# Output projection of the first 1024 tokens beside the recurrence, streamed first down product, heads in turn: a hybrid layer on one Trainium2 core

## Chip, cores and metric

The kernel runs on one core of one Trainium2 chip. The metric is the device time of one execution in microseconds (us). PE is the TensorE (matmul) engine, PEld its weight loads, DVE is VectorE, ACT is ScalarE, POOL is GpSimd, SP is SyncE, which issues most DMAs here.

## What is computed

One layer over 2048 tokens of width 1024, all in float32 at the interface. An input projection feeds three groups side by side (a diagonal state-space layer with 256 outputs, differential attention with 384, a gated linear recurrence with 384). Their 1024 outputs pass one output projection, are added to the residual, and a gated MLP (2816 wide, with a causal convolution over 3 tokens) follows.

```python
h = rmsnorm(x, norm_mix_g[l])
proj = h @ w_in[l]
u, dq, dk, dv, cq, cf, ci, cg = split_projection(proj)
y_a = s5_mixer(u, ...)                  # state space, 256 columns
y_b = diff_attention(dq, dk, dv, ...)   # 6 heads, 384 columns
y_c = hgrn2_mixer(cq, cf, ci, cg, ...)  # 6 heads, 384 columns, chunks of 64
mix = jnp.concatenate([y_a, y_b, y_c], axis=-1)
x = x + mix @ w_out[l]
h = rmsnorm(x, norm_ffn_g[l])
up, gate = h @ w_up, h @ w_gate         # up: then conv over 3 tokens + bias
x = x + (gelu(up) * gate) @ w_down
return rmsnorm(x, final_norm_g)
```

## The kernel before

**Precision.** Large products run in float16 with every operand split into a high and a low half (`Ctx.split`: one ScalarE and one VectorE or GpSimd instruction), and three of the four half products are summed. Matmuls inside the recurrence are float32.

**Two streams of work.** At the end of the kernel, `left()` yields the input projection, then attention in two halves (query tiles 0 to 7 and 8 to 15 of 128 tokens, all six heads each), and `right()` yields the state-space layer, the recurrence (`phase_hgrn`), and the rest (`phase_tail`). `weave` takes the next step from the stream whose summed price is lower. The prices are the six numbers `LW`; those of attention are also multiplied by `K.pace`, which `phase_tail` sets anew by stage. The order in which steps are drawn gives every instruction its priority. The tile framework then fixes each engine's program order when the kernel is built, from these priorities and a plan of when operands and buffers are there. An instruction further back can go first when an earlier one is not ready. `until(n)` draws attention until n head pairs are done.

**Attention.** For a head h and query tile i, `scores` issues one matmul (tile `t_ps`) and one VectorE instruction for each 512 keys and each of two maps: a score chunk. Softmax on ScalarE, a combination on VectorE, a split on ScalarE and GpSimd, transposing DMAs (`t_wt`) on SP's queue, and value matmuls (`t_po`) follow. The second half keeps fewer tiles in flight (`s_bufs` 4).

**Recurrence.** `phase_hgrn` has 12 units: three pairs of heads, four chunks of 512 tokens each. A unit is `proj` (input products, tiles `g_pq`, `g_pv`), `pre` and `fin` (which writes 128 features of 512 tokens to `Yd`). In `pre`, `meet` multiplies 64 rows of partitions (one head of the pair) for 4 blocks of 128 tokens at three levels; L1239 is its matmul. Units overlap, and the last two (10 and 11, tokens 1024 to 2047) are woven with `early_mix` under the name `spare`.

**Output projection.** `Yd` holds eight blocks of 128 features, q numbers pairs of them. `early_mix` takes q = 0, 1, 3 for tokens 0 to 511: it loads and splits six blocks of `w_out` one after another through one staging buffer (`o_wst`), then makes eight output tiles of 128 tokens by 512 columns, 18 matmuls each, in one PSUM bank (`pj`), adds x and stores the result in `Xd`. The tail's `first` adds q = 2 to those tokens (`project(0, ...)`, 48 matmuls) and does tokens 512 to 1023 whole (`project(1, ...)`, 192 matmuls). In the second half of the latter stand the transposes of the first 512 tokens (`turned(xs, left)`). The normed, transposed tokens of `first` fill seven operand tiles `f_q`.

**MLP.** `activations` makes, for half 0 (tokens 0 to 1023) and later half 1, the 22 blocks of the hidden layer. A Strassen-like scheme needs seven products instead of eight in the up projections (`f_pm`, L97), and again in the down product (class `Down`, tile `f_pd`, L1769): step i multiplies a sum of activation blocks (`f_da`, from DRAM) with a sum of blocks of `w_down` (`f_dw`), 132 matmuls a step. For half 0, steps 0 to 3 get their weights by `stage`, which loads pieces of `w_down` through three buffers (`f_dst`) and splits them. For steps 4 to 6, `hold` reserves four whole blocks of `w_down` (`f_db`), `load` fetches them, `sum` combines them on GpSimd in place, and `right` splits. `hold` uses memory of attention, so `before()` draws all attention that is left, at i = 2. `second` projects tokens 1024 to 2047; step 6 of half 0 runs inside it. The up products and the down product of half 1 follow.

In `Down.run`, with `staged` = 4 for half 0, step i prepares step i + 1:

```python
if i == staged - 1 - (staged > 1):
    before()
    self.hold(pooler(e2)("f_db", 1, side))
for b in self.LOADS[self.half].get(i, ()):
    self.load(b)
```

Of the kernel before, what the change touches and what calls it, by code (L numbers as in the profile page):

```python
# [9 lines left out]
F32 = mybir.dt.float32  # L10
# [8 lines left out]
S = 2048  # L19
# [14 lines left out]
EARLY = [0, 1, 3]  # L34
DOWN_PARTS = [3, 3, 3, 2]
MADE = range(0, MF, 2)
LW = [6.0, 0.44, 5.0, 2.5, 0.62, 1.0]
# [974 lines left out]
def phase_hgrn(K, Hd, w_in, lb_logits, norm_g, Yd, spare):  # L1012
# [9 lines left out]
    with ExitStack() as es:  # L1022
# [146 lines left out]
        def pre(u):  # L1169
# [65 lines left out]
            def meet(hl, dd, ps, e, c0):  # L1235
                hh = slice(64 * e, 64 * e + 64)
                for bk in range(NB):
                    tk = dd[hh, 128 * bk:128 * bk + 128]
                    nc.tensor.matmul(  # L1239
                        out=ps[:, c0 + 64 * bk:c0 + 64 * bk + 64].rearrange("p (n y) -> p n y", y=hl),  # L1240
                        lhsT=tk, rhs=tk.rearrange("p (n x y) -> p n x y", x=2, y=hl)[:, :, 1],
                        start=True, stop=True,
                    )
# [9 lines left out]
            for group in ((32, 16), (8,)):  # L1253
# [3 lines left out]
                for i, hl in enumerate(group):  # L1257
                    for e in range(2):
                        meet(hl, ds[i], ps[e], e, 256 * i)
# [112 lines left out]
        yield from weave(rest(), 18, spare(pj, st, wp, hp, w3, w2), 6)  # L1372


def early_mix(K, x, w_out, Yd, Xd, pj, st, wp, hp, w3, w2):

    nc = K.nc
    y = []
    for a in range(2):
        t = hp.tile([128, 2, KD, 256], F16, tag="h", name="o_ye")  # L1380
        for k in [k for q in EARLY for k in (2 * q, 2 * q + 1)]:
            nc.sync.dma_start(out=t[:, :, k], in_=Yd[k, :, :, 256 * a:256 * a + 256])
        y.append(t)
    w4 = wp.tile([128, 4, 2, 2, 512], F16, tag="w", name="o_we")
    ws = [w4[:, i] for i in range(4)]
    ws += [w2.tile([128, 2, 2, 512], F16, tag="x", name="o_wx") for _ in range(2 * len(EARLY) - 4)]
# [9 lines left out]
    for n in range(2):  # L1396
        cc = slice(512 * n, 512 * n + 512)
        for t in range(4):
            rows = slice(128 * t, 128 * t + 128)
            tk = slice(128 * (t % 2), 128 * (t % 2) + 128)  # L1400
            r = w3.tile([128, 512], F32, tag="vn", name="o_re")
            nc.sync.dma_start(out=r, in_=x[0, rows, cc])
            ps = pj.tile([128, 512], F32, tag="j", name="o_pe")
            i = 0
            for q, w in zip(EARLY, ws[len(EARLY) * n:]):
                for k in range(2):
                    for a, b in ((0, 0), (0, 1), (1, 0)):
                        nc.tensor.matmul(
                            out=ps, lhsT=y[t // 2][:, a, 2 * q + k, tk], rhs=w[:, b, k, :],
                            start=(i == 0), stop=(i == 6 * len(EARLY) - 1),  # L1410
                        )
                        i += 1
            nc.vector.scalar_tensor_tensor(
                out=r, in0=ps, scalar=IWS / YS, in1=r, op0=ALU.mult, op1=ALU.add
            )
            nc.sync.dma_start(out=Xd[S + 128 * t:S + 128 * t + 128, cc], in_=r)
            yield 1


def phase_tail(K, x, Xd, Yd, Ad, w_out, norm_g, W, conv_w, conv_b, w_down, final_g, out, es,  # L1420
# [226 lines left out]
    class Down:  # L1647
# [19 lines left out]
        LOADS = ({2: (B12, B11), 3: (B22,), 4: (B21,)}, {0: (B21,), 1: (B22, B11), 2: (B12,)})  # L1667
# [22 lines left out]
        def stage(self, i, st, cs=(0, 1, 2, 3)):  # L1690

            for c in cs:
                q0, n = self.cuts[c]
                w = self.room(i, c)
                for q in range(0, n, 2):
                    k = min(2, n - q)
                    b, pair, _ = self.STEPS[i]
                    fs = []
                    for b in pair or (b,):
# [99 lines left out]
        def run(self, rs, tp, pms, side, staged, before):  # L1799
# [3 lines left out]
            with ExitStack() as e1:  # L1803
                pool = pooler(e1)
                st = pool("f_dst", 3) if staged > 1 else None
                self.more(pool)
                if not self.w:
                    self.ahead(st)
                with ExitStack() as e2:
                    for i in range(6):  # L1810
# [3 lines left out]
                        if i == staged - 1 - (staged > 1):  # L1814
                            before()
                            self.hold(pooler(e2)("f_db", 1, side))
                        for b in self.LOADS[self.half].get(i, ()):
                            self.load(b)
                        if i + 1 < staged:
                            self.stage(i + 1, st)  # L1820
                        else:
                            for c in range(len(self.cuts)):
                                if i + 1 == staged == 4:
                                    self.sum(3, c)
                                self.right(i + 1, c)
# [3 lines left out]
                if self.half == 1:  # L1829
                    yield from self.product(6, pms[6 % len(pms)], True)  # L1830
# [284 lines left out]
```

## Time and profile before

| | us |
|---|---|
| median of three runs | 2770.08 |
| their range | 2767.73 to 2774.96 |
| the profiled execution | 2772.72 |
| its span in the profile | 2771.0 |

A row of the windows view gives, for a stretch of the span, how long each engine was busy, the clock that TensorE was granted (1.00 is full), the busy share of the DMA engines and the GB/s they moved. With a tile's name it counts only instructions that touch that tile, in the same columns for the engines that do. A row of groups gives a source line, engine, operation, names as out<-in, and count, then busy us, mean ns, and idle time before. A row of the timeline or of the chain that ended last begins with the start and the duration in us. Matmul durations overlap: 264 of some 380 ns each may pass in 60 us.

### The profile page before, as it was taken

How to read it: one execution, taken by the hardware profiler on the slowest of the kernel's cores; microseconds unless marked ns; L12 is line 12 of the kernel's file. 1: busy time of each engine (PE TensorE's matmuls, PEld its weight loads, DVE VectorE, ACT ScalarE, POOL GpSimd, SP SyncE). 2: the span in 40 equal slices, each digit the busy share in tenths (PEclk: the TensorE clock that was granted, in tenths of full speed). 3: DMA queues.
4: the chain of work that ended last, by engine and by line, in shares of the span. 5: the costliest groups of instructions: out<-in, count | busy, mean ns of one | idle time of the engine just before them, and what ended most of it. 6: DMA issues, size and time to landing. Idle time of an engine off the chain costs nothing.

```text
span 2771.0 us, 42468 instructions
## 1 busy us (share of the span) xinstructions
PE 2437.1 (88%) x15438; PEld 1374.1 (50%) x15438; DVE 1941.6 (70%) x3497; ACT 1269.5 (46%) x2273; POOL 1362.6 (49%) x1144
## 2 busy tenths in 40 slices
PE   5998889988988888868987988769999999999998
PEld 4655547766766764334443433334344444444444
DVE  7567746888878987688778998963654755555475
ACT  6333344666645654654455665541234433333221
POOL 5787602544444543456667566622902444444280
PEclk8999999988998888879999989979999999999999
DMA  7676554555464656954456555687675655554733
GB/s 245 228 224 194 179 155 112 125 125 123 86 153 97 129 131 142 296 143 129 171 158 177 159 161 146 211 238 239 229 266 178 227 156 150 167 156 135 282 101 122
DMA packets 554531, 474.11 MB, mean 171 GB/s; under 512 B 276880, under 2 KB 432848, under 8 KB 553296
## 3 DMA queue, kind: packets, MB, share of 16 engines
q1 hardware_dynamic: 532144, 431.02, 55.1%
q10 hardware_dynamic: 22176, 40.38, 4.0%
q8 instruction: 121, 1.98, 0.3%
q14 instruction: 90, 0.74, 0.1%
HBM read 289.30 MB, written 127.93 MB: 151 GB/s over the span
## 4 chain that ended last, share of the span: by engine, by line
PE 36%; DVE 15%; DMA 9%; issue 8%; ACT 6%; POOL 5%; SPq 1%; ACTq 0%; DVEq 0%; POOLq 0%
PE f_pm L97 15%; PE f_pd L1769 10%; PE o_pm L1486 3%; DVE t_sc L837 3%; DMA t_wt<-t_sc 2%; DVE t_sc L868 2%; ACT t_sc L849 2%; DMA f_dst<-in_w_down_dram 2%; PE g_pq L97 2%; DMA o_y<-Yd 1%; PE g_pv L97 1%; POOL t_sc L892 1%; DVE f_w L64 1%; DVE f_t L1610 1%; DVE f_a L62 1%
## 5 line engine op out<-in xcount | busy, mean ns | idle before, releaser
L97 PE MATMUL f_pm<-f_q,f_w 128*128 128x512 f16 x3696 | 844.3, 388 | 43.3 <-DVE f_u L1834 24.9
L97 PEld LDWEIGHTS <-f_w 128*128 128x128 f16 x3696 | 364.3, 100 | 501.1 <-issue 80.5
L1769 PE MATMUL f_pd<-f_dw,f_da 128*128 128x512 f16 x1848 | 408.7, 384 | 15.1 <-DVE f_r L1747 10.2
L892 POOL TENSOR_TENSOR t_sc<-t_sc 128x1024 f16<-128x1024 f32 (+7 forms) x144 | 253.6, 1774 | 278.8 <-ACT t_sc L891 220.9
L1769 PEld LDWEIGHTS <-f_da 128*128 128x128 f16 x1848 | 182.4, 99 | 238.0 <-issue 23.0
L849 ACT ACTIVATE t_sc<-t_sc,t_nm 128x128 f32<-128x128 f32 (+7 forms) x192 | 229.0, 1194 | 77.7 <-DVE t_nm L844 69.8
L833 PE MATMUL t_ps<-t_k,t_q 96*128 96x512 f16 (+2 forms) x480 | 167.3, 374 | 93.0 <-DVE t_mx L837 84.1
L837 DVE CUSTOM_DVE_ANT_0 t_sc<-t_ps,t_base,t_mx 128x512 f32<-128x512 f32 (+3 forms) x288 | 185.2, 645 | 26.9 <-PE t_ps L833 17.1
L62 DVE TENSOR_TENSOR f_a<-f_t,f_a 128x512 f16<-128x512 f32 x132 | 158.3, 1219 | 50.1 <-ACT f_a L56 49.6
L914 PEld LDWEIGHTS <-t_wt 128*128 128x128 f16 x2448 | 107.9, 103 | 117.7 <-DMA t_wt<-t_sc 50.1
L868 DVE SCALAR_TENSOR_TENSOR t_sc<-t_sc,t_a 128x1024 f32<-128x1024 f32 (+7 forms) x144 | 164.9, 1170 | 1.1
L97 PE MATMUL g_pv<-g_w,g_h 128*128 128x256 f16 x1152 | 157.1, 294 | 9.1 <-ACT g_w L56 8.1
L1834 POOL TENSOR_TENSOR f_t<-f_t,f_t 128x512 f32<-128x512 f32 x66 | 101.9, 1557 | 126.9 <-ACT f_a L56 91.6
L1486 PE MATMUL o_pm<-o_w,o_y 128*128 128x512 f16 x624 | 144.1, 389 | 20.8 <-DMA o_y<-Yd 10.4
L97 PE MATMUL g_pq<-g_h,g_w 128*128 128x256 f16 x1152 | 156.7, 292 | 6.0 <-DVE g_sg L1161 3.9
L914 PE MATMUL t_po<-t_v,t_wt 128*128 128x64 f16 x2448 | 122.6, 200 | 40.7 <-DMA t_wt<-t_sc 35.4
L1834 POOL TENSOR_TENSOR f_db<-f_db 128x1536 f32<-128x1536 f32 (+1 forms) x32 | 128.1, 4041 | 56.0 <-DMA f_db<-in_w_down_dram 56.0
L64 DVE SCALAR_TENSOR_TENSOR f_dw<-f_db,f_dw 128x1536 f16<-128x1536 f32 (+1 forms) x36 | 103.3, 2898 | 71.7 <-ACT f_dw L56 71.7
L891 ACT CAST t_sc<-t_sc 128x1024 f16<-128x1024 f32 (+7 forms) x144 | 111.2, 793 | 86.6 <-DVE t_sc L868 82.9
L1834 POOL TENSOR_TENSOR f_k<-f_k,f_k 128x512 f32<-128x512 f32 x88 | 124.6, 1416 | 51.0 <-ACT f_halo L1878 25.2
L1610 DVE SCALAR_TENSOR_TENSOR f_t<-f_u,f_cw,f_t 128x1024 f32<-128x1024 f32 x88 | 125.8, 1429 | 32.6 <-ACT f_t L1608 32.3
L837 DVE CUSTOM_DVE_ANT_0 t_sc<-t_ps,t_base 128x512 f32<-128x512 f32 (+2 forms) x192 | 120.8, 633 | 37.7 <-PE t_ps L833 19.1
(327 smaller groups left out, 4463.1 us busy)
## 6 DMA issues: line engine op xcount, KB each, us to landing
f_w<-Wd SPq DMA_DIRECT2D x231, 256.0 KB, 2.9
Wd<-f_w SPq DMA_DIRECT2D x154, 256.0 KB, 2.1
Ad<-f_a ACTq DMA_DIRECT2D x154, 256.0 KB, 2.6
f_da<-Ad SPq DMA_DIRECT2D x42, 768.0 KB, 4.5
g_h<-Hd SPq DMA_DIRECT2D x24, 1024.0 KB, 6.8
f_db<-in_w_down_dram SPq DMA_DIRECT2D x24, 768.0 KB, 8.7
o_wst<-in_w_out_dram SPq DMA_DIRECT2D x32, 512.0 KB, 5.4
o_y<-Yd SPq DMA_DIRECT2D x52, 256.0 KB, 4.5
```

Of the source, the lines that this page charges most:

```text
L62: nc.vector.tensor_tensor(out=lo, in0=src, in1=hi, op=ALU.subtract)
L97: nc.tensor.matmul(out=out, lhsT=lhs(a, k), rhs=rhs(b, k), start=(n == 0), stop=(n == 3 * nk - 1))
L833: nc.tensor.matmul(out=ps[:, 0:k1 - k0], lhsT=qt[:, c, 128 * (i % 4):128 * (i % 4) + 128], rhs=H.k[:, c, k0:k1], start=True, stop=True,)
L837: V.tensor_tensor_reduce(out=sc[c][:, k0:k1], in0=ps[:, 0:k1 - k0], in1=bs[:, k0:k1], scale=1.0, scalar=-3e38 if j == 0 else mx[:, c, j - ...
L849: nc.scalar.activation(out=sc[c][:, 0:L], in_=sc[c][:, 0:L], func=AF.Exp, scale=SLOPES[h], bias=nm[:, c:c + 1], accum_out=H.la[:, c, n_:n_ ...
L868: V.scalar_tensor_tensor(out=sc[0][:, k0:k1], in0=sc[1][:, k0:k1], scalar=a[:, 1:2], in1=sc[0][:, k0:k1], op0=ALU.mult, op1=ALU.add,)
L892: nc.gpsimd.tensor_tensor(out=hl[:, LM + k0:LM + k1], in0=sc[0][:, k0:k1], in1=hl[:, k0:k1], op=ALU.subtract,)
L914: nc.tensor.matmul(out=po, lhsT=wt[:, w, b, :], rhs=vt[:, b, 64 * v:64 * v + 64], start=(b == 0 and w + v == 0), stop=(b == i and w == 1),)
L1486: nc.tensor.matmul(out=ps[t], lhsT=y[:, k, a, 128 * t:128 * t + 128], rhs=w[:, b, k, :], start=(q == qs[0] and i == 0), stop=(q == qs[-1] ...
L1610: V.scalar_tensor_tensor(out=t0, in0=u[:, c:n + c], scalar=cw[:, c, m:m + 1], in1=t0, op0=ALU.mult, op1=ALU.add,)
L1769: nc.tensor.matmul(out=ps[t], lhsT=a[:, q, x, tk], rhs=w[:, y, q, :], start=(first and q + x + y == 0), stop=(last and q == n - 1 and y == 1),
L1834: eng.tensor_tensor(out=o, in0=a, in1=b, op=op)
```

## The change

1. **Heads in turn.** `meet` issues the matmuls of the two heads of a pair alternately, block by block, instead of four and four.
2. **Output projection of the first 1024 tokens.** `early_mix` waits for `until(3)` and takes all four q for tokens 0 to 511 and then 512 to 1023: eight blocks of `w_out`, 16 output tiles of 24 matmuls. It also sums their squares on ScalarE into `ss`, which lives in the constant pool. `first` loads the finished rows and only scales and transposes them. `EARLY`, the two `project` calls and the two `keep` calls of `first` go. The weave of `rest` and `spare` goes from 18:6 to 18:16.
3. **Streamed first down product.** For half 0, all seven steps get their weights by `stage`, now with four buffers. One block, `kept`, stays in memory between step 5 and step 6. `before()` is called at i = 4. `run` serves half 1 alone, as before.
4. **Prices.** `LW[4]` goes from 0.62 to 0.72, and `K.pace` in the up products of half 0 from 1.0 to 0.86.

```diff
-EARLY = [0, 1, 3]
-LW = [6.0, 0.44, 5.0, 2.5, 0.62, 1.0]
+LW = [6.0, 0.44, 5.0, 2.5, 0.72, 1.0]
...
-            def meet(hl, dd, ps, e, c0):
-                hh = slice(64 * e, 64 * e + 64)
+            def meet(hl, dd, ps, c0):
                 for bk in range(NB):
-                    tk = dd[hh, 128 * bk:128 * bk + 128]
-                    nc.tensor.matmul(
...
+                    for e in range(2):
+                        tk = dd[64 * e:64 * e + 64, 128 * bk:128 * bk + 128]
+                        nc.tensor.matmul(
+                            out=ps[e][:, c0 + 64 * bk:c0 + 64 * bk + 64].rearrange(
...
-        yield from weave(rest(), 18, spare(pj, st, wp, hp, w3, w2), 6)
+        more = pool("o_z", 1)
+        yield from weave(rest(), 18, spare(more, pj, st, wp, hp, w3, w2), 16)
...
+def early_mix(K, x, w_out, Yd, Xd, ss, more, pj, st, wp, hp, w3, w2):
...
     ws = [w4[:, i] for i in range(4)]
+    ws += [more.tile([128, 2, 2, 512], F16, tag=f"z{i}", name="o_wz") for i in range(2)]
+    ws += [w2.tile([128, 2, 2, 512], F16, tag="x", name="o_wx") for _ in range(2)]
     for i, w in enumerate(ws):
-        n, q = divmod(i, len(EARLY))
-        q = EARLY[q]
+        n, q = divmod(i, 4)
         f = st.tile([128, 2, 512], F32, tag="wst", name="o_wst")
...
+    for c in range(2):
+        y = []
+        for a in range(2):
+            t = hp.tile([128, 2, KD, 256], F16, tag="h", name="o_ye")
+            t0 = CH * c + 256 * a
+            for k in range(KD):
+                nc.sync.dma_start(out=t[:, :, k], in_=Yd[k, :, :, t0:t0 + 256])
+            y.append(t)
+        for n in range(2):
+            cc = slice(512 * n, 512 * n + 512)
+            for t in range(4):
+                rows = slice(CH * c + 128 * t, CH * c + 128 * t + 128)
...
+                r = w3.tile([128, 512], F32, tag="vn", name="o_re")
+                nc.sync.dma_start(out=r, in_=x[0, rows, cc])
+                ps = pj.tile([128, 512], F32, tag="j", name="o_pe")
...
+                sq = more.tile([128, 512], F16, tag="sq", name="o_sq")
+                nc.scalar.activation(
+                    out=sq, in_=r, func=AF.Square, scale=D ** -0.5, accum_out=ss[:, c, n, t:t + 1]
+                )
+                nc.sync.dma_start(out=Xd[rows, cc], in_=r)
+                yield 1
...
+        SUMS = (
+            (B11,), (B21,), (B22,), (B12, B11), (B22, B12), (B22, B12, B11), (B21,),
+        )
+
+        def stage(self, i, st, kept=None):
...
                     f = fs[0]
-                    if pair:
+                    if i == 6:
+                        add(f, kept[:, q0 + q:q0 + q + k], f, ALU.subtract, P)
+                    elif len(fs) > 1:
                         add(f, f, fs[1], ALU.subtract, P)
+                    if i == 5:
+                        t = kept[:, q0 + q:q0 + q + k]
+                        add(t, f, fs[2])
+                        f = t
                     K.split(w[:, 0, q:q + k], w[:, 1, q:q + k], f, WS)
...
+        def streamed(self, rs, tp, pm, before):
...
+                st = pool("f_dst", 4)
+                self.more(pool)
+                self.ahead(st)
+                kept = None
+                for i in range(6):
+                    for c in range(len(self.cuts)):
+                        if (i, c) not in self.a:
+                            self.left(i, c)
+                    if i == 4:
+                        before()
+                        kept = e1.enter_context(
+                            tc.tile_pool(name="f_db", bufs=1, side="left", reuse_waits="tile")
+                        ).tile([128, MF // 2, CH], F32, name="f_db")
+                    self.stage(i + 1, st, kept)
+                    yield from self.product(i, pm, False)
+            self.last = self.product(6, pm, False)
...
-                r0, r1 = [], []
-                s0, s1 = sums(), sums()
-                yield from project(
-                    0, [q for q in range(4) if q not in EARLY], st, wp, yp, (pm,), onto(r0, s0, tp),
-                    lambda: r0.extend(residual(rp, Xd[S:S + CH])))
+                r0, r1 = [residual(rp, Xd[CH * c:CH * c + CH]) for c in range(2)]
                 xs = spread(hc, 1) + spread(hc, 3)
-                keep(r0, 0)
-                scaled(r0, xs, s0)
-                yield from project(1, range(4), st, wp, yp, (pm,), onto(r1, s1, tp),
-                                   lambda: r1.extend(residual(rp, x[0, CH:N])),
-                                   turned(xs, (pm,), left))
-                keep(r1, CH)
-                scaled(r1, r1, s1)
+                scaled(r0, xs, ss[:, 0])
+                scaled(r1, r1, ss[:, 1])
+                yield from turned(xs, (pm,), left)
                 yield sum(turned(r1, (pm,), right))
-            K.pace = 1.0
+            K.pace = 0.86
             yield from activations(hc, 0, pooler(e1), pm, 1, 3, 5, 3, None)
...
-        yield from down.run(total(0), tp, [pm], "left", 4, ahead)
+        yield from down.streamed(total(0), tp, pm, ahead)
...
             def spare(*pools):
-                until(2)
-                yield from early_mix(K, x, w_out, Yd, Xd, *pools)
+                until(3)
+                yield from early_mix(K, x, w_out, Yd, Xd, ss, *pools)
```

More of the change, by code (lines that the diff above doesn't have):

```diff
@@ L1257, in pre @@
                 for i, hl in enumerate(group):
-                    for e in range(2):
-                        meet(hl, ds[i], ps[e], e, 256 * i)
+                    meet(hl, ds[i], ps, 256 * i)
                 for e in range(2):
@@ L1395, in early_mix @@
         K.split(w[:, 0], w[:, 1], f, WS)
[L1396 to L1417, printed above, removed]
@@ L1420, in phase_tail @@
-def phase_tail(K, x, Xd, Yd, Ad, w_out, norm_g, W, conv_w, conv_b, w_down, final_g, out, es,
+    for c in range(2):
[10 more added lines that the diff above has]
+                rows = slice(CH * c + 128 * t, CH * c + 128 * t + 128)
+                tk = slice(128 * (t % 2), 128 * (t % 2) + 128)
+                r = w3.tile([128, 512], F32, tag="vn", name="o_re")
+                nc.sync.dma_start(out=r, in_=x[0, rows, cc])
+                ps = pj.tile([128, 512], F32, tag="j", name="o_pe")
+                i = 0
+                for q in range(4):
+                    for k in range(2):
+                        for a, b in ((0, 0), (0, 1), (1, 0)):
+                            nc.tensor.matmul(
+                                out=ps, lhsT=y[t // 2][:, a, 2 * q + k, tk],
+                                rhs=ws[4 * n + q][:, b, k, :], start=(i == 0), stop=(i == 23),
+                            )
+                            i += 1
+                nc.vector.scalar_tensor_tensor(
+                    out=r, in0=ps, scalar=IWS / YS, in1=r, op0=ALU.mult, op1=ALU.add
+                )
+                sq = more.tile([128, 512], F16, tag="sq", name="o_sq")
+                nc.scalar.activation(
+                    out=sq, in_=r, func=AF.Square, scale=D ** -0.5, accum_out=ss[:, c, n, t:t + 1]
+                )
+                nc.sync.dma_start(out=Xd[rows, cc], in_=r)
+                yield 1
@@ L1421, in phase_tail @@
+def phase_tail(K, x, Xd, ss, Yd, Ad, w_out, norm_g, W, conv_w, conv_b, w_down, final_g, out, es,
                ahead):
@@ L1688, in room @@
             return w
-        def stage(self, i, st, cs=(0, 1, 2, 3)):
-            for c in cs:
-                q0, n = self.cuts[c]
+        SUMS = (
+            (B11,), (B21,), (B22,), (B12, B11), (B22, B12), (B22, B12, B11), (B21,),
+        )
+        def stage(self, i, st, kept=None):
+            for c, (q0, n) in enumerate(self.cuts):
                 w = self.room(i, c)
@@ L1696, in stage @@
                     k = min(2, n - q)
-                    b, pair, _ = self.STEPS[i]
                     fs = []
-                    for b in pair or (b,):
+                    for b in self.SUMS[i]:
                         f = st.tile([128, KD, 128], F32, tag="wst", name="f_dst")
@@ L1797, in product @@
                 yield 2.5 * self.cuts[c][1]
-        def run(self, rs, tp, pms, side, staged, before):
+        def streamed(self, rs, tp, pm, before):
             self.rs, self.tp = rs, tp
@@ L1804, in run @@
                 pool = pooler(e1)
-                st = pool("f_dst", 3) if staged > 1 else None
+                st = pool("f_dst", 4)
                 self.more(pool)
-                if not self.w:
-                    self.ahead(st)
+                self.ahead(st)
[12 more added lines that the diff above has]
+            self.last = self.product(6, pm, False)
+        def run(self, rs, tp, pms, side):
+            self.rs, self.tp = rs, tp
+            with ExitStack() as e1:
+                pool = pooler(e1)
+                self.more(pool)
                 with ExitStack() as e2:
@@ L1813, in run @@
                                 self.left(i, c)
-                        if i == staged - 1 - (staged > 1):
-                            before()
+                        if i == 0:
                             self.hold(pooler(e2)("f_db", 1, side))
-                        for b in self.LOADS[self.half].get(i, ()):
+                        for b in self.LOADS.get(i, ()):
                             self.load(b)
[L1819 to L1825, printed above, removed]
+                        for c in range(len(self.cuts)):
+                            self.right(i + 1, c)
                         if i < 5:
@@ L1828, in run @@
                 yield from self.product(5, pms[5 % len(pms)], False)
-                if self.half == 1:
-                    yield from self.product(6, pms[6 % len(pms)], True)
-            self.last = self.product(6, pms[0], False)
+                yield from self.product(6, pms[6 % len(pms)], True)
     def add(o, a, b, op=ALU.add, eng=V):
@@ L1996, in phase_tail @@
     eh.close()
-    yield from down.run(total(1), tp, [pd, pm], "left", 1, lambda: None)
+    yield from down.run(total(1), tp, [pd, pm], "left")
 @with_exitstack
```

26 lines of the change are left out of this document (8 added, 18 removed).

## The prediction

> **What bounds it now.** First the engines' busy shares, then windows cut at the stages.
>
> ```profile
> span 2771.0 us, 42468 instructions
> PE 2437.1 (88%) x15438; PEld 1374.1 (50%) x15438; DVE 1941.6 (70%) x3497; ACT 1269.5 (46%) x2273; POOL 1362.6 (49%) x1144
> ```
> ```profile
> 445.00:790.00 345.00, 304.87 (x3109) 247.75 (x3110) 277.11 (x750) 203.68 (x508) 152.93 (x138) 0.90 0.55 117
> 790.00:1010.00 220.00, 192.21 (x1914) 150.05 (x1913) 185.50 (x461) 125.90 (x214) 98.06 (x75) 0.87 0.55 118
> 1010.00:1096.00 86.00, 75.26 (x642) 47.90 (x641) 68.41 (x157) 39.83 (x70) 35.05 (x25) 0.88 0.57 142
> 1096.00:1221.00 125.00, 91.88 (x595) 47.48 (x594) 89.47 (x173) 72.18 (x127) 49.12 (x30) 0.83 0.90 238
> 1221.00:1829.00 608.00, 497.50 (x2822) 231.39 (x2822) 518.20 (x770) 340.33 (x552) 390.32 (x251) 0.90 0.56 160
> 1829.00:2027.00 198.00, 181.52 (x847) 81.45 (x847) 102.92 (x96) 49.80 (x65) 82.66 (x27) 0.96 0.71 239
> 2172.00:2771.00 599.00, 590.57 (x2724) 267.00 (x2723) 328.82 (x374) 186.08 (x291) 254.26 (x168) 0.99 0.52 165
> ```
>
> Columns: window, length, busy PE, PEld, DVE, ACT, POOL, granted clock, DMA share, GB/s. The windows are the recurrence beside the first attention half (445), then beside the second (790), the early projection (1010), the rest of the first projection with norm and transposes (1096), the up products of half 0 (1221), its down product (1829) and the second half's products (2172). The last runs at 99% of PE and is not edited. From 445 to 1829 no engine is full: PE is at 74 to 88%, DVE at 72 to 85%, and attention runs beside everything. Down (1829) has DVE at 52% and no attention scores, as the next rows show.
>
> Score chunks of attention (tile t_ps), same windows and two of 70 us, columns PE, DVE, clock, DMA; then the up products (f_pm) with PE, DVE, ACT:
>
> ```profile
> 790.00:1010.00 220.00, 40.20 (x112) 74.74 (x112) 0.87 0.55 118
> 1010.00:1096.00 86.00, 10.72 (x30) 19.51 (x30) 0.88 0.57 142
> 1221.00:1829.00 608.00, 55.82 (x149) 100.37 (x152) 0.90 0.56 160
> 1829.00:2027.00 198.00, 0.00 (x0) 0.00 (x0) 0.96 0.71 239
> 1330.00:1400.00 70.00, 0.33 (x1) 0.00 (x0) 1.00 0.50 175
> 1610.00:1680.00 70.00, 6.92 (x20) 13.89 (x21) 0.89 0.58 163
> ```
> ```profile
> 1330.00:1400.00 70.00, 67.50 (x312) 10.28 (x15) 5.52 (x10) 1.00 0.50 175
> 1610.00:1680.00 70.00, 55.69 (x218) 7.32 (x11) 4.29 (x8) 0.89 0.58 163
> ```
>
> Without attention 312 up matmuls pass in 70 us, with 20 chunks 218. So 20 chunks cost 94 matmuls x 70/312 = 21 us: **1.05 us a chunk** while up products run.
>
> **Part 1, heads in turn.** The g_pl matmuls (L1239) run four for one head, then four for the other; the g_pb ones (L1280) already alternate.
>
> ```profile
> L1239 PE MATMUL g_pl<-g_d 64*128 64x64 f32 x576 | 69.2, 297 | 0.0
> L1280 PE MATMUL g_pb<-g_e 64*128 64x128 f32 x192 | 19.6, 316 | 8.5 <-DVE g_e L1273 8.5
> ```
> ```profile
> 1014.08 1.16 PE L1280 MATMUL g_pb<-g_e 64*128 64x128 f32 x16
> ...
> 1035.47 2.00 PE L1239 MATMUL g_pl<-g_d 64*128 64x64 f32 x16
> ```
>
> Sixteen alternating ones take 1.16 us, though they move twice the columns; sixteen in sequence 2.00. 576 are 36 such groups: 36 x 1.16 = 42 us against 69.2, so 27 us of PE less; by the mean of g_pb (19.6/12 = 1.63 a group) only 10. PE is 88% busy there, but DVE 80 to 84%, so only part arrives. I take -8; ends 0 and -27. Both banks must now be free at a group's first matmul; I price that at nothing, as g_pb has the same need, within the same ends.
>
> **Part 2, projection beside the recurrence.** 240 matmuls (48 and 192) leave the first projection, and 240 join the early one (144 to 384): PE work is equal. Gone are eight w_out loads and splits, the stores and reloads of the sums (keep), and the startup. What stays behind the last eviction, in the chain that ended last and in PE's order of time:
>
> ```profile
> 1193.08 0.69 DVE o_r L1499
> ...
> 1221.74 3.41 PE f_pm L97 x8
> ```
> ```profile
> 1161.46 0.60 PE L1530 MATMUL o_pt<-ident,f_q 128*128 128x128 f32 x4
> ...
> 1169.11 0.66 PE L1530 MATMUL o_pt<-ident,f_q 128*128 128x128 f32 x4
> ```
> ```profile
> L64 DVE SCALAR_TENSOR_TENSOR o_we<-o_wst,o_we x4: 1211/1410/1835, 1017.3 to 1046.7; 128x1024 f16<-128x1024 f32 x4
> L1413 DVE SCALAR_TENSOR_TENSOR o_re<-o_pe,o_re x8: 677/689/692, 1048.5 to 1096.2; 128x512 f32<-128x512 f32 x8
> ```
>
> Until(3) is met like until(2): all chunks from 790 on are the second half's, so the first half's third pair is written. The first tile needs four weight pairs, and the fourth is split at 1046.7 + 1.4, so it leaves its bank at about 1052. Eight evictions now lie 47.7/7 = 6.8 us apart with 18 matmuls; six more at 0.226 (row of the 264 below) make 8.2 us. For the last eight the recurrence is over: 24 x 0.226 + 0.69 + 1 for handover = 7.1. 1052 + 7 x 8.2 + 8 x 7.1 = 1166. Token chunk 1's 16 Yd loads and all x loads and stores stand in SP's queue between attention's transposes; two tiles of time cover them. Square sums go to ScalarE, under half busy.
>
> What lay inside project(1) is now bare: scaling (I allow 4 us: twice the 1.4 us of a 128x1024 split on two engines, and rsqrt), the left transposes (1161.46 to 1169.77: 8 us), then from last eviction to first up product 1193.1 to 1221.7: 28.6. The store and reload of the last rows hide behind the left transposes. 1166 + 41 = 1207 against 1221.7: -15. The fit is tight, since one us more a tile costs 15; I take -10, ends -18 (all tiles 7.1 and a first tile at 1048) and +27 (10 us each).
>
> A stretch like this bare one stands in the present kernel:
>
> ```profile
> 1190.00:1260.00 70.00, 41.60 (x275) 23.29 (x273) 66.59 (x123) 41.89 (x83) 42.12 (x27) 0.71 0.53 137
> ```
>
> The clock granted was 0.71, against 1.00 in 1330:1400. If 41 bare us go at 0.71, 0.29 x 41 = 12 us are lost; I leave it to rival 1, as transposes and attention do not fill PE there. [...]
>
> **Part 3, priorities.** The order between the two streams is by weights. From 790 to 1096 attention's price rises from 0.62 to 0.72: 142 chunks x 0.14 = 20 fewer. Eight more mix steps x 2.5 / 0.72 = 28 units, at 56 chunks per 212 units 7 more. In `first`, 66 / (1.8 x 0.62) = 59 units become 16 / (1.8 x 0.72) = 12: 12 fewer. Net 25 chunks later. In the up products 0.86 x 0.72 = 0.62, as before. So 25 chunks fall into Down, worth 25 x 1.05 = 26 us before it. As attention also runs ahead of its place wherever engines idle, I take -20; ends -26 and 0. Down pays PE for 25 chunks: a score matmul of 6.92/20 = 0.35 and some five value matmuls (three to a key block) of 1.07/31 (the x31 row below), 0.52 together, 13 us, half of it in Down's present gaps: +6.
>
> **Part 4, streamed down.**
>
> ```profile
> 1930.33 14.24 DMA f_db<-in_w_down_dram
> ```
> ```profile
> 1967.76 59.76 PE f_pd L1769 x264
> ```
> ```profile
> 1894.05 1.07 PE L914 MATMUL t_po<-t_v,t_wt 128*128 128x64 f16 x31
> ```
> ```profile
> 1930.86 30.34 PE L1769 MATMUL f_pd<-f_dw,f_da 128*128 128x512 f16 x132 [3.68 <-DVE f_r L1747]
> 1967.76 2.72 PE L1769 MATMUL f_pd<-f_dw,f_da 128*128 128x512 f16 x6 [6.56 <-DVE f_r L1747]
> ```
> ```profile
> L1834 POOL TENSOR_TENSOR f_dst<-f_dst x7: 1260/2342/2348, 1887.9 to 1925.5; 128x1024 f32<-128x1024 f32 x4, 128x512 f32<-128x512 f32 x3
> ```
> ```profile
> f_dst<-in_w_down_dram SPq DMA_DIRECT2D x24, 512.0 KB, 4.9
> ```
> ```profile
> 1830.00:1890.00 60.00, 56.37 (x262) 25.14 (x261) 30.77 (x37) 18.22 (x21) 6.42 (x3) 0.95 0.81 252
> 1925.00:1960.00 35.00, 31.32 (x139) 13.76 (x137) 5.56 (x6) 2.60 (x3) 21.73 (x8) 0.95 0.99 368
> ```
>
> Two gaps, 3.7 and 6.6 us, come from holding raw weights in memory that attention frees late: 10 us go. In place come 77 pieces against 42 and 16 loads. The worst is stage 5, three sources a piece with four buffers: 4.9 + 2.3 (POOL) + about 1.2 (DVE add, as a split) = 8.4, x 4, and three half-size at 6 = 52 us. Its room opens with product 4, and the last cut is needed one product (30) and three quarters (22) later: it just fits. But `kept` waits for attention, which is flushed two products later (last t_po now 1895, so about 1955): some 7 us, and 3 for crowding. Net 0, ends -10 and +25 (each piece 3.5 us longer). Pieces came at 252 GB/s, held blocks at 368; at 252 stage 5 with its operands (8.65 and 2.88 MB) takes 46 us, inside the 52.
>
> [...]
>
> **Sum.** -8 - 10 - 20 + 6 + 0 = -32 on the profiled run's own 2772.7 (span 2771.0 and 1.7 around it): 2740.7. The median of the three runs, 2770.1, lies 2.6 lower, so 2738.
>
> **Rivals.**
> 1. Idle is moved, not removed. The bare 41 us run at low clock (+12), and attention, already ahead, leaves nothing for Down (+15): 2765. For: 0.71; PE idle in 1190:1260 is 28 us. Against: 1330:1400 shows up products taking back full speed at once.
> 2. Slower: the mix has one PSUM bank (g_pj), so each tile waits for its eviction and for x behind SP's transposes. At 10.7 us a tile instead of 7.6, 15 x 3.1 = 46 more: 2784. It decides from 10.3 on. For: the eight tiles took 79 us from first matmul (1017), 9.9 each. Against: most of that was the wait for weights.
> 3. More: part 1 gives 27 rather than 8 and part 3 all 26: 2713.
> 4. The streamed stages stall on their pieces (+25): 2763. For: 252 against 368 GB/s. Against: 252 is what stages 1 to 3 draw now, with PE busy 56 of 60 us.
>
> **Chances.** Forecast 0.53; rival 1 0.16; rival 2 0.14; rival 3 0.12; rival 4 0.05. About 0.3%, 8 us, is what a measurement tells from no change: faster 0.70, same 0.16, slower 0.14. The range goes from below rival 3, 2703, to rival 2's edge, 2782.
>
> **What would show it.** Sixteen g_pl matmuls near 1.2 us; evictions of the mix 7 to 8 us apart; first f_pm near 1205; t_ps in Down, and the up stage under 608 us; Down near 200 us without a gap over 7 us; from the first f_pm of half 1 on, the same 599 us. I am wrong if mix tiles take 10 us, if the up stage is no shorter, or if products 4 and 5 wait for f_dst.

## The result and the profile after

| | us |
|---|---|
| before, median of five runs beside it | 2772.22 (2767.73 to 2774.96) |
| after, median of five runs | 2756.50 (2750.61 to 2761.92) |
| ratio after to before | 0.9931, 95% interval 0.991 to 0.9953 |
| profiled execution after (before) | 2750.61 (2772.72) |
| its span (before) | 2748.9 (2771.0) |

The change makes the kernel 0.7% faster (15.7 us between the medians, 22.1 between the profiled executions). The forecast was 2738, which is 1.2%: between half (by the medians) and six tenths (by the ratio) of it arrived.

The head of the profile after, and its windows, cut at the same events as before (columns as before):

```profile
span 2748.9 us, 42509 instructions
PE 2429.6 (88%) x15438; PEld 1365.9 (50%) x15438; DVE 1924.5 (70%) x3497; ACT 1255.9 (46%) x2270; POOL 1357.3 (49%) x1149
```

```profile
445.00:770.00 325.00, 290.70 (x3103) 236.46 (x3102) 265.29 (x746) 200.83 (x506) 152.69 (x138) 0.92 0.57 123
770.00:989.00 219.00, 185.73 (x1885) 147.50 (x1882) 179.26 (x428) 114.83 (x200) 91.69 (x72) 0.86 0.49 108
989.00:1091.00 102.00, 92.79 (x654) 54.51 (x653) 73.58 (x154) 48.45 (x86) 35.91 (x25) 0.75 0.62 160
1091.00:1197.00 106.00, 80.22 (x542) 44.28 (x540) 70.97 (x160) 60.11 (x106) 36.57 (x24) 0.86 0.71 174
1197.00:1794.00 597.00, 492.60 (x2737) 226.34 (x2737) 512.87 (x752) 325.79 (x536) 401.80 (x255) 0.91 0.56 164
1794.00:2004.00 210.00, 198.91 (x1063) 92.45 (x1062) 115.65 (x161) 64.13 (x92) 71.91 (x34) 0.95 0.83 263
2156.00:2749.00 593.00, 585.45 (x2712) 265.15 (x2710) 322.41 (x367) 184.78 (x286) 253.81 (x167) 1.00 0.51 163
```

PE is still busy for 88% of the span, with the same number of matmuls: nothing was taken away, things were moved. The stretch beside the first attention half is 325 us long (345 before) and the up stage 597 (608). The stage Down, the first down product, is however 210 us (198), and PE is busy for 95% of it (92%).

The score chunks of attention (t_ps; PE, DVE, clock, DMA share, GB/s) in the up stage and in Down, after:

```profile
1197.00:1794.00 597.00, 54.77 (x142) 93.56 (x142) 0.91 0.56 164
1794.00:2004.00 210.00, 5.37 (x17) 13.84 (x20) 0.95 0.83 263
```

Before, these were 149 and none. Seventeen chunks, with all that follows each of them, now lie in Down. The forecast had 25 there.

For every kernel of this study I took the trace's start of the recurrence's first product, of the first f_pm of half 0, of the first f_pd, of the last f_pd of Down's product 5, of the first f_pm of half 1 and of the last f_pd. Their differences are the stages below (us). That first product starts anywhere from 393.2 to 399.4 in these profiles, though the work ahead of it isn't edited; so lengths are compared and not starts. Each row is one profile: the seven kernels that have the same edits up to Down (after, no_stream, flush2, flush3 and the last three) differ by up to 7.2 us in the first column and 1.2 in the next.

| kernel | recurrence, mix, first | up, half 0 | Down | second | half 1 | 
|---|---|---|---|---|---|
| before | 828.3 | 607.6 | 198.0 | 130.8 | 605.1 |
| after | 803.2 | 596.3 | 210.6 | 137.2 | 599.6 |
| heads_only | 817.7 | 604.6 | 197.3 | 135.6 | 604.1 |
| proj_only | 814.7 | 617.3 | 196.7 | 137.5 | 603.5 |
| heads_proj | 796.0 | 615.9 | 196.7 | 136.8 | 601.1 |
| stream_only | 826.4 | 608.8 | 204.4 | 123.5 | 607.6 |
| no_heads | 809.9 | 601.2 | 209.5 | 134.0 | 602.9 |
| no_stream | 807.0 | 596.0 | 238.4 | 135.9 | 603.2 |
| old_prices | 801.1 | 614.9 | 197.0 | 132.8 | 600.6 |
| flush2 | 806.1 | 596.3 | 200.4 | 148.2 | 600.3 |
| flush3 | 799.8 | 596.6 | 206.1 | 145.3 | 600.7 |
| y3 | 804.0 | 596.3 | 211.7 | 131.5 | 599.8 |
| y_once | 802.6 | 595.6 | 209.6 | 129.0 | 600.9 |
| y_once_flush3 | 801.8 | 595.4 | 208.7 | 128.3 | 600.8 |

Of the 36.4 us that after has gained when Down begins (25.1 and 11.3), Down and the second projection give back 19.0 (12.6 and 6.4). The question is which part of the change gained, and why the rest went.

The border between Down and the second projection isn't sharp: some matmuls of the second projection (o_pm, 384 in all) run inside Down, and the work counts there. The o_pm matmuls inside Down, in old_prices, after, flush2 and flush3 (PE busy, count, DVE, clock, DMA share, GB/s):

```profile
1815.40:2012.30 196.90, 3.78 (x16) 0.00 (x0) 0.96 0.83 276
1793.70:2004.20 210.50, 8.85 (x38) 0.00 (x0) 0.95 0.83 263
1800.40:2000.80 200.40, 1.89 (x8) 0.00 (x0) 0.97 0.87 279
1792.80:1998.90 206.10, 3.78 (x16) 0.00 (x0) 0.95 0.82 266
```

Before has none, and stream_only 26. So the two columns are safest read together.

### The profile page after: what moved, and what is told of

It reads as the page before. It is cut to its first block, busy times and chain, and to the rows that moved or that the text cites. A ratio compares the mean times of both kernels' runs of the same rounds, so it can differ in the third digit from the quotient of the medians.

```text
span 2748.9 us, 42509 instructions
## 1 busy us (share of the span) xinstructions
PE 2429.6 (88%) x15438; PEld 1365.9 (50%) x15438; DVE 1924.5 (70%) x3497; ACT 1255.9 (46%) x2270; POOL 1357.3 (49%) x1149
## 5 line engine op out<-in xcount | busy, mean ns | idle before, releaser
L96 PE MATMUL f_pm<-f_q,f_w 128*128 128x512 f16 x3696 | 839.2, 387 | 34.5 <-DVE f_u L1863 10.4
L867 DVE SCALAR_TENSOR_TENSOR t_sc<-t_sc,t_a 128x1024 f32<-128x1024 f32 (+7 forms) x144 | 180.5, 1279 | 1.3
L96 PE MATMUL g_pq<-g_h,g_w 128*128 128x256 f16 x1152 | 149.7, 288 | 10.4 <-DVE g_sg L1160 5.4
L96 PEld LDWEIGHTS <-g_h 128*128 128x128 f16 x1152 | 118.0, 104 | 50.6 <-issue 22.5
L55 ACT ACTIVATE f_a<-f_t 128x512 f16<-128x512 f32 x154 | 94.8, 627 | 96.4 <-DVE f_a L61 32.1
L55 ACT ACTIVATE f_w<-f_sum 128x512 f16<-128x512 f32 x110 | 69.1, 628 | 150.0 <-DVE f_sum L139 65.1
```

The source lines that it names most:

```text
L55: nc.scalar.activation(out=hi, in_=src, func=AF.Copy, scale=scale)
L96: nc.tensor.matmul(out=out, lhsT=lhs(a, k), rhs=rhs(b, k), start=(n == 0), stop=(n == 3 * nk - 1))
L867: V.scalar_tensor_tensor(out=sc[0][:, k0:k1], in0=sc[1][:, k0:k1], scalar=a[:, 1:2], in1=sc[0][:, k0:k1], op0=ALU.mult, op1=ALU.add,)
```

## Experiments

Each was timed in five rounds. The kernels of one group ran on one chip with the same runs of before, whose medians were 2775.6 (first group), 2771.1 (second) and 2772.7 (third), so kernels are compared by their ratios. All compute the whole layer.

### Which part is worth what

**heads_only**: the kernel before with the new `meet` alone.

```diff
                 for bk in range(NB):
-                    tk = dd[hh, 128 * bk:128 * bk + 128]
+                    for e in range(2):
+                        tk = dd[64 * e:64 * e + 64, 128 * bk:128 * bk + 128]
```

> The kernel before with the heads in turn alone (the 64-row products of the two heads of a pair issued alternately). Theory H (the heads are most of the gain: with everything joined the recurrence's input products end 23.7 us earlier and the first half of attention 20 us earlier): recurrence's last input product ends about 1013 - 20 = 993 us, time about 2772 - 18 = 2754 (2750 to 2759). Rival P (my prediction's size, 8 us; the rest of the 24 us comes from the dearer price of attention and the joined projection): last input product about 1005, time about 2764 (2760 to 2768). If alternating does nothing: 2772.

Measured: ratio 0.9971 (0.9956 to 0.9987), 8 us of 2772. By the time, the rival, which is my forecast's own size, was right, and theory H wrong; the recurrence's last input product (g_pv) starts at 999.9 us, between the 993 and the 1005 of the two. The row of groups of the g_pl matmuls, in heads_only:

```profile
L1239 PE MATMUL g_pl<-g_d 64*128 64x64 f32 x576 | 54.5, 291 | 0.0
```

It was 69.2 us before: 14.7 us of PE went, of which 8 arrived. In the table 13.6 us are gained when Down begins, and the second projection, 135.6 in place of 130.8, gives 4.8 back. **no_heads**, the kernel after with the old `meet`:

> The kernel after with the two heads of a pair in sequence again. Theory H: the recurrence's last input product comes back from 989 to about 1010 us, time about 2756.5 + 18 = 2774, no better than before. Rival P: about 1000 us and 2764; the price of attention and the projection would then keep their share without the heads.

Measured: 0.9977 (0.996 to 0.9995) against 0.9931 for after; the heads are worth 0.46% or 13 us there, with the widths of both intervals on it. 0.9977 x 2772 is 2766, near rival P's 2764, and the last input product starts at 999.6. A timeline of PE shows the groups of 16, first in no_heads and then in after:

```profile
502.13 1.60 PE L1238 MATMUL g_pl<-g_d 64*128 64x64 f32 x16
```

```profile
499.96 1.11 PE L1238 MATMUL g_pl<-g_d 64*128 64x64 f32 x16
```

The gain is 0.5 us in this group, and 14.7 / 36 = 0.4 in the mean. I had read 2.00 for a group in sequence from one row at 1035 us. The granted clock was 1.00 there too (before, 1035.47 to 1037.50), as in after's row and at before's own group at 499.40 us, which took 1.60, so the clock doesn't explain that row, and what made it slow was not tried. By the rows of no_heads and after the edit could give 36 x 0.49 = 17.6, not 27.

**proj_only**: the kernel before with the joined projection alone (part 2 of the change, with the old prices).

```diff
-        yield from weave(rest(), 18, spare(pj, st, wp, hp, w3, w2), 6)
+        more = pool("o_z", 1)
+        yield from weave(rest(), 18, spare(more, pj, st, wp, hp, w3, w2), 16)
...
-                until(2)
-                yield from early_mix(K, x, w_out, Yd, Xd, *pools)
+                until(3)
+                yield from early_mix(K, x, w_out, Yd, Xd, ss, *pools)
```

> The kernel before with the joined projection alone (1024 tokens beside the recurrence; held blocks, old prices, heads in sequence). If the terms add up (heads in turn 8 us, heads in turn with the projection 16 us, streaming and prices together nothing): 2772 - 8 = 2764 (2760 to 2768). Rival (the projection needs the gaps that the heads in turn opened, or takes its 17 us of the first f_pm without giving any back): 2772, or 2756.

Measured: 1.0025 (1.001 to 1.004), slower by 7 us; the terms don't add up here. Its profile can't show these 7 us: that run took 2773.97, near the low end of its twelve (2773.05 to 2784.5), and its stages sum to what before's do. **heads_proj** joins it to the heads in turn, with held blocks and the old prices:

> Heads in turn and the joined projection alone: held blocks and the old prices as before. Theory S: as quick as with the streamed form at the old prices, ratio 0.992 to before, 2750 to 2756; then the whole gain is these two. Rival G (streaming is worth 10 us or more at any price): ratio 0.996, 2762 or more.

Measured: 0.9941 (0.9924 to 0.9958). The time, 0.9941 x 2772 = 2756, is the upper end of theory S's, but the ratio lies as near to rival G's 0.996 as to S's 0.992, so this run alone doesn't decide between them; stream_only below does. The projection gains some 8 us beside the heads in turn (0.9971 to 0.9941; the intervals just overlap) and costs 7 without them. The score chunks in the up stage of before, proj_only, heads_only and heads_proj, in that order:

```profile
1221.50:1829.10 607.60, 55.48 (x149) 99.87 (x151) 0.90 0.56 161
```

```profile
1209.10:1826.40 617.30, 59.11 (x153) 103.34 (x156) 0.90 0.54 159
```

```profile
1211.50:1816.10 604.60, 56.51 (x147) 99.03 (x149) 0.91 0.55 161
```

```profile
1195.10:1811.00 615.90, 61.54 (x153) 103.51 (x156) 0.90 0.55 160
```

In both pairs the projection lets the up stage start early (13.6 and 21.7 us by the table), with four to six more chunks left for it, and the stage is 9.7 and 11.3 us longer. At the prediction's 1.05 us a chunk, the chunks are 4 to 6 us of that. What is left at the first f_pd is 3.9 us alone and 10.4 with the heads; alone, the second projection then takes 6.7 us more than before. Why the pair gains more at the first f_pm than the two alone (32.3 against 10.6 + 13.6) stays open: old_prices, which has the same work up to there, gains 27.2, so up to 5 us of it differs from one profile to the next.

**stream_only**: the kernel before with the streamed Down alone.

```diff
-        down = Down(0, pooler(el))
-        yield from down.run(total(0), tp, [pm], "left", 4, ahead)
+        yield from down.streamed(total(0), tp, pm, ahead)
```

> The kernel before with the streamed first product down alone (old prices, heads in sequence, old projection). Theory S (streaming is worth nothing while attention ends before Down's product 4; its large worth of 33 us beside the dear prices, 2789.6 against 2756.5, is there because the held form must have attention's memory at product 3): first f_pd to half 1's first f_pm 329 us as before, time 2772 (2768 to 2776). Rival G (held blocks cost gates of 10 us whatever the prices): 2762.

Measured: 1.0006 (0.999 to 1.0023), no change, as forecast; rival G's 2762 falls. From the first f_pd to the first f_pm of half 1 it is 327.9 us, before 328.8. Pieces of 512 and 256 KB (f_dst, which in before took 4.9 and 4.1 us to land, in the median) in place of 768 and 512 KB ones (f_db, 8.7 and 11.1 us there) cost nothing that these intervals show: in Down, PE waited 2.2 us for f_dst, before 3.6.

**old_prices**: the kernel after with LW[4] and K.pace as before.

```diff
-LW = [6.0, 0.44, 5.0, 2.5, 0.72, 1.0]
+LW = [6.0, 0.44, 5.0, 2.5, 0.62, 1.0]
...
-            K.pace = 0.86
+            K.pace = 1.0
```

> The kernel after with the old prices (attention 0.62, pace of the following stage 1.0). Theory: the dearer prices moved only some 9 score chunks out of the up stage (8 us), and in Down they let attention end 33 us later than the kept adds are due; with the old prices the up stage is 8 us longer and Down some 10 to 18 us shorter: 2750 to 2757. Rival (my prediction: the prices are worth 20 us in the up stage and cost 6 in Down): about 2770.

Measured: 0.992 (0.9899 to 0.9942), as quick as after (0.991 to 0.9953). So beside the other three parts the prices are worth nothing that these intervals show, and the rival, my forecast's sum, falls. Windows of old_prices, then of after, over up stage, Down and second projection:

```profile
1200.50:1815.40 614.90, 497.75 (x2818) 229.10 (x2817) 523.19 (x788) 348.81 (x563) 402.62 (x258) 0.92 0.56 160
1815.40:2012.30 196.90, 185.77 (x908) 84.79 (x908) 104.81 (x120) 56.59 (x79) 67.69 (x33) 0.96 0.83 276
2012.30:2145.10 132.80, 119.52 (x567) 56.64 (x566) 65.41 (x92) 55.86 (x101) 30.12 (x25) 0.97 0.66 234
```

```profile
1197.40:1793.70 596.30, 492.30 (x2737) 226.25 (x2737) 512.17 (x752) 325.09 (x535) 401.44 (x255) 0.91 0.56 164
1793.70:2004.20 210.50, 199.41 (x1064) 92.63 (x1064) 116.15 (x161) 64.43 (x92) 72.11 (x34) 0.95 0.83 263
2004.20:2141.50 137.30, 117.64 (x545) 55.14 (x544) 80.02 (x109) 62.97 (x117) 44.64 (x31) 0.94 0.65 231
```

This is where the expected gain went. The dear prices shorten the up stage by 18.6 us, of which 5.4 is PE's work and 13.2 its idle time. Down becomes 13.6 longer, and PE is busy 13.6 us more in it (199.41 against 185.77): PE's idle time there is 11.1 us in both, so no gap took anything in. This work is attention's and, also the second projection's. Busy times by tile rise by 5.4 us for t_ps (none to 17), 6.2 for t_po (93 to 210) and, in the rows of the section before, 5.1 for o_pm (16 to 38); they overlap in part, so they aren't to be summed. The second projection, with 22 matmuls fewer left to do, is even so 4.5 us longer: PE is idle 19.7 us in place of 13.3. Its wait for o_y grew by 3.8 (10.2 to 14.0), and the last wait before half 1, for f_r, by 2.5 (3.1 to 5.6). Up stage, Down and second projection together are 944.6 and 944.1.

**no_stream**: the kernel after with held blocks (part 3 undone, the dear prices kept).

> The kernel after with the first product down on held blocks again (streaming undone; heads, projection, prices stay). Theory K (the streamed form costs: from the first f_pd to half 1's first f_pm 347.8 us after against 328.9 before, because stage 5's kept adds wait for the last attention step at 1957 us): about 2756.5 - 15 = 2741 (2737 to 2746). Rival A (the 18.9 us are attention's TensorE work that the dearer price moved into this stage, and come whatever the form): 2756 (2752 to 2760). Rival G (holding blocks costs its gates, 10 us, as I wrote for before): about 2766.

Measured: 1.0043 (1.0027 to 1.0058), slower than before and 31 us slower than after (0.0112 x 2772). All three theories gave a wrong number. The largest wait of PE from Down's start to the first f_pm of half 1 (us, times, longest), then the timelines of PE and of SP's queue:

```profile
PE f_pd L1776 <- ACT f_dw L55: 36.5, 2, 35.1
```

```profile
1973.67 3.29 PE L1776 MATMUL f_pd<-f_dw,f_da 128*128 128x512 f16 x8 [35.07 <-ACT f_dw L55]
```

```profile
1942.39 0.52 SPq L948 DMA_DIRECT2D Yd<-t_yo  x1
1943.00 22.98 SPq L1730 DMA_DIRECT2D f_db<-in_w_down_dram  x16
```

Attention's last output leaves at 1942.39, and right behind it the loads of the held blocks start, in memory that attention had. Sums and splits follow the loads, and product 4 waits 35 us for all this. At the old prices attention is over early enough (heads_proj: Down 196.7). So streaming is worth nothing by itself, and some 31 us beside the dear prices: it takes away a wait that, among these kernels, only they make.

### Is it the kept block, or attention's own work?

In after, the chain that ended last passes through attention's last steps into the first add to `kept` (start, us, what):

```profile
1955.61 0.70 ACT t_yo L55
1956.33 0.76 DVE t_yo L63
1957.12 1.24 DVE f_db L1863
1958.37 0.39 SPq L1713
```

The block is f_db; the add holds a staging buffer, and the next load of a piece (L1713) goes out behind it. I took this for the cause of Down's longer time. **flush2** and **flush3** draw the rest of attention two steps or one earlier, with `kept` reserved where it was:

```diff
-                    if i == 4:
+                    if i == 2:
                         before()
+                    if i == 4:
                         kept = e1.enter_context(
```

> The kernel after with the rest of attention drawn behind product 2 of the streamed Down (as the held form did) and no longer behind product 4; the kept block's place in memory is reserved where it was. Theory K (the kept adds wait at 1929 to 1957 us for attention's last step, and products 4 and 5 take 38.2 and 36.7 us for that): attention ends some 20 us earlier, the sum from the first f_pd to half 1's first f_pm falls from 347.8 to about 335, time 2756.5 - 13 = 2743 (2740 to 2748). Rival A (attention's own TensorE work, some 14 us, is the cost, wherever in Down it lies): about 348 again and 2756 (2753 to 2759).

> The kernel after with the rest of attention drawn behind product 3 and no longer behind product 4. Theory K: half of what drawing it behind product 2 brings, 2749 (2744 to 2753). Rival A: 2756.

Measured: 0.9942 (0.9924 to 0.9959) and 0.9943 (0.9924 to 0.9962), both as after. Theory K is wrong: rival A's 2756 came, and the sum from the first f_pd to half 1's first f_pm is 348.6 and 351.4 us, where rival A had 348. Down does get shorter (200.4 and 206.1 against 210.6), but not by a wait: PE's idle time in it is 10.7 and 10.9 us, against 11.1. PE's work in it is 9.7 and 4.2 us less, and most of that is o_pm matmuls (8 and 16 in place of 38, 7.0 and 5.1 us by the rows further up), which the second projection now has to do. It takes 148.2 and 145.3 us in place of 137.2, of which PE's work is 7.7 and 4.1 and idle time 3.2 and 3.9. What PE waited for there, first in after, then in flush2 and in flush3 (us, times, longest):

```profile
PE o_pm L1493 <- DMA o_y<-Yd: 14.0, 5, 5.6
```

```profile
PE o_pm L1493 <- DMA o_y<-Yd: 17.2, 5, 5.8
```

```profile
PE o_pm L1493 <- DMA o_y<-Yd: 17.9, 5, 8.0
```

`second` loads its operand blocks from `Yd` (o_y) through two buffers, and each twice, once for each half of the columns. Its matmuls wait 14 us for them in after, and 3.2 and 3.9 us longer in flush2 and flush3. That is all that its idle time grew by; the rest of its extra length is the work passed on.

### Taking that wait away

**y3** gives it three buffers; **y_once** loads each block once, into four buffers, and has two weight buffers and not three; **y_once_flush3** adds the earlier drawing of flush3.

```diff
-            yp, wp, st = pool("o_y2", 2, "left"), pool("f_w2", 3, "left"), pool("f_st2", 2, "left")
+            yp, wp, st = pool("o_y2", 4, "left"), pool("f_w2", 2, "left"), pool("f_st2", 2, "left")
...
+        ys = {}
         for n in range(2):
...
-                y = yp.tile([128, 2, 2, CH], F16, tag="y", name="o_y")
-                for k in range(2):
-                    nc.sync.dma_start(out=y[:, k], in_=Yd[2 * q + k, :, :, j * CH:(j + 1) * CH])
+                if n == 0:
+                    ys[q] = yp.tile([128, 2, 2, CH], F16, tag="y", name="o_y")
+                    for k in range(2):
+                        nc.sync.dma_start(out=ys[q][:, k], in_=Yd[2 * q + k, :, :, j * CH:(j + 1) * CH])
+                y = ys[q]
```

> The kernel after with three o_y buffers in the second projection and not two. Theory W (the second projection gives back what Down gains, because its products wait for the o_y transfers: 14.0 us after, 17.2 with attention drawn behind product 2, 10.8 with heads and projection alone): the waits fall to some 7 us, time 2749 (2746 to 2754). Rival C (TensorE's work is what counts, and these waits only make room for other waits, or the transfers are bound by the rate): 2756 (2753 to 2759).

> The kernel after with each o_y block loaded once for both column halves (four buffers, 16 transfers and not 32; two weight buffers and not three). Theory W: the waits for o_y fall under 4 us, time 2746 (2742 to 2752). Rival C: 2756. Rival B (the third weight buffer is needed, and o_w's splits come late in its place): 2758 or more.

> The same with the rest of attention drawn behind product 3. Theory W: now the 10 us by which Down became shorter stay, 2740 (2736 to 2747), clearly under the one before. Rival C: the same as the one before within 4 us.

Measured: y3 2746.04 us, 0.9915 (0.9894 to 0.9937); y_once 2745.27, 0.991 (0.9895 to 0.9926); y_once_flush3 2740.41 (2732.47 to 2745.73), 0.9889 (0.987 to 0.9909). Waits of PE in the second projection, in y3 and then in y_once:

```profile
PE o_pm L1493 <- DMA o_y<-Yd: 6.2, 3, 3.9
...
PE o_pm L1493 <- DVE o_w L63: 4.3, 1, 4.3
```

```profile
PE o_pm L1496 <- ACT o_w L55: 8.1, 2, 5.8
...
PE o_pm L1496 <- DVE o_w L63: 1.0, 1, 1.0
```

The wait for o_y falls from 14.0 to 6.2 and then goes, and part comes back as a wait for the split weights, 5.1 (0.8 of it for ACT's half) and 9.1 us, so rival B has its share. The second projection takes 131.5 and 129.0 us in place of 137.2, 6 to 8 us less; the ratios fall by 4 to 6 us, though their intervals overlap with after's. The clear pair is flush3 and y_once_flush3, 0.9943 (0.9924 to 0.9962) against 0.9889: there loading once takes 15 us off, the intervals don't meet, and the second projection falls from 145.3 to 128.3. PE's idle time from the first f_pd to half 1's first f_pm falls from 34.4 to 23.5 us. So theory W holds in that the o_y waits cost time which can be had. It doesn't hold in that they took a gain of Down's back: most of what Down lost was work passed on. Whether drawing attention earlier adds anything to y_once isn't settled: 337.0 us against 338.6 for Down and second projection together, medians 5 us apart, intervals that overlap. y_once_flush3 is the fastest here, 1.1% under before, with an interval wholly under after's. Whether the dear prices pay beside it was not tried.

## Why the forecast was right or wrong

**Heads in turn, -8: right.** Alone they measure 8 us, in the joined change 13. The upper end, 27, rested on one slow row; what PE's busy time really lost was 14.7.

**Projection, -10: right in size, with a condition I hadn't seen.** The evictions of the mix, in the kernel after:

```profile
L1416 DVE SCALAR_TENSOR_TENSOR o_re<-o_pe,o_re x16: 677/691/692, 1035.7 to 1150.8; 128x512 f32<-128x512 f32 x16
```

That is 115.1 / 15 = 7.7 us a tile, inside the 7.1 to 8.2 of the sum; rival 2 asked for 10.7 and fell. The first tile came 16 us before the forecast 1052, as the recurrence was earlier, and the first f_pm at 1197.4 for 1207. The low clock of the bare stretch came as forecast, between the last eviction and the first f_pm and behind it:

```profile
1151.00:1197.00 46.00, 26.42 (x218) 18.95 (x216) 39.98 (x84) 38.24 (x62) 25.66 (x16) 0.72 0.77 214
1197.00:1267.00 70.00, 53.95 (x292) 24.30 (x292) 66.11 (x99) 38.57 (x67) 51.84 (x32) 0.79 0.48 122
```

Before has such a stretch too, 0.66 in the 28 us from 1193 and 0.82 in the 70 behind it. Length times missing clock is 22.1 us there and 27.6 here, so by this estimate at most 5 or 6 of rival 1's 12 us came. But the clock behind the first f_pm is 0.79, not 1.00: the argument against rival 1, that the up products take back full speed at once, was read from a window that begins some 100 us behind the first f_pm. One end was also summed wrongly: a first tile 4 us sooner and seven tiles 1.1 us shorter are 12 beyond the -10, so -22 and not -18.

**Prices: this step failed, and it is the miss.** The -20 before Down was near: by the table, old_prices to after, up to the first f_pd, 1416.0 to 1399.5, 16.5 us. The step that failed is "+6", with its reason "half of it in Down's present gaps". From the first f_pd to the first f_pm of half 1 it measured 18.1 (329.7 to 347.8). In Down PE's work grew by 13.6, and none of it went into gaps. That this is the 13 of the sum is luck: the sum had 25 chunks of 0.52, and 17 came, which is 9, while 22 o_pm matmuls that the sum didn't have came with them. The other 4.5 came in a place that I hadn't priced, the second projection behind Down, where PE idled 6.4 us more. Rival 1's title, idle is moved, fits this, and 2756.5 lies nearer to its 2765 than to the forecast. Its mechanism doesn't: it had attention leave nothing for Down, and 17 chunks came.

**Streamed Down, 0: right by itself, misjudged as a part.** Alone it is 1.0006. But 0 was a sum of -10 for the held gates and +10 for waits, and neither came as priced, so the 0 is in part luck. The rows of the two gaps name f_r, an eviction on DVE, and not the held blocks; ahead of the first of these evictions DVE was splitting a staged piece, not a held block:

```profile
1928.98 1.23 DVE L64 SCALAR_TENSOR_TENSOR f_dw<-f_dst,f_dw 128x1024 f16<-128x1024 f32 x1 [5.09 <-ACT f_dw L56]
1930.12 2.48 DVE L1747 SCALAR_TENSOR_TENSOR f_r<-f_pd,f_r 128x512 f32<-128x512 f32 x4
```

Ahead of the second, of 6.6 us, it was splitting held blocks (f_dw<-f_db, 8.4 us from 1958.06), so at most that one was the held form's. Without held blocks, in stream_only, PE still waits 8.3 us for f_r in Down (10.2 before), and its idle time there is 17.6 us (16.5 before). Where held blocks did gate, in no_stream, PE waited 35.1 us, behind attention's last output at 1942.39 us. The add to `kept` came at 1957 us, as forecast, but its price of 7 us isn't seen: drawing attention earlier left PE's idle time in Down as it was. The edits that meet in Down can't be summed one by one. Rival 4 fell: among PE's waits in after's Down none is for f_dst.

**The sum.** In the profiled runs -38 was forecast before Down, and -36.4 came; +6 behind that, and +19.0 came. Half 1, which isn't edited, took 599.6 in place of 605.1, and these 5.5 us of the 22.1 were not forecast; it lies between 599.6 and 601.1 in all kernels with both heads and projection but no_stream (603.2), and at 602.9 to 607.6 in the others. What sets it was not tried. The medians of five runs lie 15.7 us apart and the two profiled runs 22.1; the ratio stands for 19.

## What to carry to other kernels

Before work is moved from one stage to another, read PE's idle time in the stage that receives it: at 94% busy (185.77 of 196.9 us) the moved work was paid in full. When a stage ends sooner, count what ran in it: if PE's idle time is the same and only its work is less, the work has been passed on, as the o_pm matmuls were in flush2. Then look at what the next stage waits for; here that wait, 14 to 18 us for o_y, was worth more than the earlier end. And price two edits that share a memory or a deadline together: streaming was worth nothing alone, and 31 us once another edit made attention late.

## What I had not expected of the hardware

In after, the granted clock was 0.75 from 989 to 1091 us although PE was busy for 91% of that window (92.79 of 102); in the unedited kernel's 1010 to 1096 it was 0.88 at 88%. A busy share read from the profile did not tell the clock there. Inside the window the clock was 1.00 up to 994 us, 0.50 for the 47.8 us behind that, and 0.97 from 1041.8 on. The middle one (columns as in the windows above):

```profile
994.00:1041.80 47.80, 43.25 (x221) 25.40 (x220) 40.18 (x83) 26.07 (x37) 22.43 (x15) 0.50 0.67 159
```

PE's longest idle time in it is 2.85 us. What lowered the clock was not tried. The same instructions were busy for longer at the low clock: sixteen g_pl matmuls in sequence took 1.60 us at a granted clock of 1.00 (before, at 499.40 us) and 2.88 at 0.50 (at 1002.19). So part of a busy share read at 0.50 is the low clock itself.
